# Turning the value tiles with one VectorE transpose and 24 ScalarE copies

## Chip, core and metric

The kernel runs on one core of a Trainium2 chip. The metric is the device time of one launch in microseconds; it is the median of the runs shown. PE is TensorE's matmul, PEld its weight load, DVE VectorE, ACT ScalarE, SP the engine that issues most DMAs.

## What is computed

One layer of a decoder trunk, for 256 new tokens of a prompt and for 8 sequences of 8 new tokens with a carried state: 320 tokens in all, model width 2048, fp32. Two token mixers read one input projection: A is an mLSTM with 4 heads (keys 256 wide, values 512), B an HGRN2 recurrence with 8 heads (keys 128, values 256). Cut to what matters here:

```python
proj = jnp.einsum('btd,de->bte', x, w_in)          # ml_q, ml_k, ml_v, ..., hg_q, hg_f, hg_i, hg_g, gate_a, gate_b
h, C, n, m = _mlstm(q, k, v, ig, lf, C0, n0, m0)   # num = (q k^T * d) v + w q C
branch_a = layernorm(h) * ml_norm_g * sigmoid(ml_o)
o, S = _hgrn2(hq, log f, 1 - f, hg_i, S0)          # o = a i + (q exp(G)) S
branch_b = rmsnorm(o) * hg_norm_g * silu(hg_g)
merged = sigmoid(gate_a) * (branch_a @ w_a) + sigmoid(gate_b) * (branch_b @ w_b)
x1 = layernorm(alpha * x + merged @ w_out)
y = layernorm(alpha * x1 + relu(x1 @ w_up)**2 @ w_down)
```

`v` and `hg_i` come out of the projection with channels on the partitions and tokens along the free dimension. The products with the score matrices need them with tokens on the partitions. That turn is what the change touches.

## The kernel before

**Projection stream.** All weights are cut into tiles of 128 output columns (`TILES`, L40): 40 tiles for the four heads of A (four `mv`, two `mk`, two `mq` and two gate tiles each), 4 gate tiles, 48 tiles for the eight heads of B (two gate tiles, `hf`, `hq` and two `hi` each), 16 `o` tiles, 4 gate tiles, then the branch, output and feed-forward tiles. A tile is two units of 8 blocks; each block is three matmuls of 320 columns (weights hi times x hi, hi times x lo, lo times x hi; L531 to L533), so a unit is 24 matmuls and a tile 48. The exact fp32 product is made of such hi and lo parts.

**Weight units.** SP loads a unit (128x1024) into `wr`. ACT rounds it to the hi part (L494, shown under the helper's line L350), DVE subtracts it to get the lo part (L497). There are three hi and lo buffers (`HL`), so a unit's conversion can start when PE has finished the unit three before it.

**Side work.** Everything else is done by chains: Python generators that yield one instruction at a time with an engine and a cost. While the program is built, a planner (`Sched`, L144 to L242) keeps a clock for each engine and lets a chain issue when its inputs are ready and the engine's queue is short. ACT and DVE instructions may be issued at most 0.9 us ahead of PE's clock; side matmuls go in between the projection's. So the costs in the program (`dve_t`, L269, is that of a transpose) set the order in which instructions stand on every engine, and nothing else: on the chip each engine works through its own row in order and waits only for real inputs.

**The turn.** `turn` (L1145) takes a value tile `x` (128 channels x n tiles x 320 tokens; n is 4 in A, `m_V` L948, and 2 in B, `h_i` L1474) and writes `to` with tokens on the partitions. A DVE transpose turns 32x32 blocks where they stand, so each group of 32 channel rows and 32 token columns must also change its partition quarter. Before, 24 transposes on 32 partitions do both: 16 for the prompt (L1156) and 8 for the sample tokens (L1159). Afterwards ACT and DVE make hi and lo parts of the turned values (L963 in A; L1487 and L1488 in B), and a matmul with `spread` copies the sample rows to where the state update needs them.

**Output rows.** In `h_out` (L1615) the two 128x256 halves of a head's prompt output are normalised, each is turned in place (L1631), and four DMAs write them home.

**The o tiles.** `ev_o` (L1691) makes branch A: the sigmoid of a tile read from its PSUM bank (L1309 to L1316), the product with the head output fetched from DRAM (L1698), then the split in hi and lo parts (L1672), the lo part into `ra`. In `ra`, the places for tile 7 and later are the same bytes that the last heads of B still use for their scan (`phl`) and their state update (`hkz0`). Three PSUM banks (`mbank`) take turns for the projection; ev_o holds one of two buffers (`sg`) from its first instruction to its split.

**Names in the rows.** `wh` and `wl` are hi and lo weights, `xh` and `xl` hi and lo x; `f`, `f3h`, `rx`, `ra`, `rxb`, `bb`, `rh` are big SBUF areas of which chains hold parts; `misc` holds single columns. Helpers give all ACT instructions the line L350 and most matmuls L356.

Of the kernel before, what the change touches and what calls it, by code (L numbers as in the profile page):

```python
# [20 lines left out]
TOK = 320  # L21
KT = 16
MH, DK, DV = 4, 256, 512
HH, HK, HV = 8, 128, 256
# [220 lines left out]
def wait(*evs):  # L245
    return ("wait", evs)


def acq(pool, n=1):
    return ("acq", pool, n)  # L250


def rel(pool, item):
    return ("rel", pool, item)


def post(ev):
    return ("set", ev)


def act(n, psum=False, ptr=0):
    return ((61 if psum else 112) + n) / 1.2 + 93 * ptr


def dve(n, psum=False, mode=1, ptr=0):
    return ((62 if psum else 66) + n / mode) / 0.96 + 55 * ptr


def dve_t(n):  # L269
    return 155.0 + 1.07 * n  # L270


def pe_f(n, m=128):
    return max(212.0 if m == 128 else 162.0, n * 1.66)
# [20 lines left out]
def by_row(ap, off, gap):  # L295

    return cap(ap, off, [[32, 4], [8, 2], [1, 8]] if gap else [[8, 4], [32, 2], [1, 8]])
# [16 lines left out]
class Program:  # L314
# [674 lines left out]
    def m_KW(self, h):  # L989
# [13 lines left out]
        m["khl"] = khl  # L1003
        kh, kl = khl[:, 0], khl[:, 1]
        yield ("dve", dve_t(512), lambda: v.transpose(kw[:, :, 0:256], kw[:, :, 0:256]))
        yield ("act", act(512), lambda: self.A(kh.rearrange("p s k -> p (s k)").rearrange("p (c t) -> p c t", c=2), kw[:, :, 0:256]))
        yield ("dve", dve(512), lambda: v.tensor_tensor(kl, kw[:, :, 0:256], kh.bitcast(F32), ALU.subtract))
# [56 lines left out]
    def m_num(self, h):  # L1064
# [14 lines left out]
        for i in range(2):  # L1079
            b = yield acq(self.sbank)  # L1080
            jobs = [(c, s) for c, s in (((0, 0),), ((128, 0), (256, 1)))[i]]
            n = 0
            for c, s in jobs:
                for x, w in ((sh, vh), (sh, vl), (sl, vh)):
                    st, sp = n == 0, n == 3 * len(jobs) - 1
                    yield ("pe", pe_r(512), lambda: self.mm(b, x[:, c:c + 128], w[:, s, :], start=st, stop=sp))
                    n += 1
            yield from self.ln_post(h, i, b, db[:, i:i + 1], hb[:, i, :], 128, True)
            yield rel(self.sbank, b)
            yield ("dve", dve_t(512), lambda: v.transpose(hb[:, i, :], hb[:, i, :]))  # L1090
# [54 lines left out]
    def turn(self, to, x):  # L1145

        v = self.nc.vector
        n = x.shape[1]
        for a in range(4):
            p = slice(32 * a, 32 * a + 32)  # L1150
            col = lambda y: y.rearrange("p (c a k) -> p a c k", a=4, k=32)[:, a]
            for b in range(4):
                q = slice(32 * b, 32 * b + 32)
                i = x[p, :, 0:NP_].rearrange("p c (i b k) -> p b i c k", b=4, k=32)[:, b]
                o = to[q, 0:2, :].rearrange("p i (c a k) -> p a i c k", a=4, k=32)[:, a]
                yield ("dve", dve_t(64 * n), lambda: v.transpose(o, i))  # L1156
            for b in range(2):
                o, i = col(to[64 + 32 * b:96 + 32 * b, 2, :]), x[p, :, NP_ + 32 * b:NP_ + 32 * b + 32]
                yield ("dve", dve_t(32 * n), lambda: v.transpose(o, i))  # L1159

    def later(self):
        e = Ev()
# [452 lines left out]
    def h_out(self, h):  # L1615
        nc, v, m = self.nc, self.nc.vector, self.hh[h]
        if h:
            yield wait(self.hh[h - 1]["o"])
        yield wait(m["aT"], m["I"])
        at, it = m["at"], m["it"]  # L1620
        on = yield acq(self.on)
        yield post(m["o"])
        b = yield acq(self.sbank)
        yield ("pe", pe_f(256), lambda: self.mm(b[:, 0:256], at[:, 0:128], it[:, 0, :], start=True, stop=True))
        yield ("pe", pe_f(256), lambda: self.mm(b[:, 256:512], at[:, 368:496], it[:, 0, :], start=True, stop=False))
        yield ("pe", pe_f(256), lambda: self.mm(b[:, 256:512], at[:, 128:256], it[:, 1, :], start=False, stop=True))
        for i in range(2):
            yield from self.rms(b[:, 256 * i:256 * i + 256], on[:, i, :], 128)
        yield rel(self.sbank, b)
        for i in range(2):  # L1630
            yield ("dve", dve_t(256), lambda: v.transpose(on[:, i, :], on[:, i, :]))  # L1631
        yield from self.place(self.rows_to(self.oH[h]), on[:, 0:2, :].rearrange("p i v -> p (i v)").rearrange("p (b c) -> p b c", c=32))
        done = self.later()
        yield wait(m["S"])
        ob = m["ob2"]
        yield from self.rms(ob[:, 0:256], on[:, 2, :], 128)
        yield rel(self.sbank, ob)
        yield rel(self.at, at)
        b = yield acq(self.sbank)
        for j in range(2):  # L1640
            yield ("pe", PE_T, lambda: nc.tensor.transpose(b[:, 128 * j:128 * j + 128], on[:, 2, 128 * j:128 * j + 128], self.ident))
        o = yield acq(self.ho)
        for j in range(2):
            yield ("act", act(64, True), lambda: self.A(by_row(o, 64 * j, False), by_row(b, 128 * j, True)))
        yield rel(self.sbank, b)
        yield ("sp", 620, lambda: self.dma(
            self.oL[h].rearrange("(j p) t -> p j t", p=128), o[:, 0:128].rearrange("p (j t) -> p j t", t=64)))
        for j in range(2):
            yield post(self.oT_ev[2 * h + j])
        yield wait(self.later())  # L1650
        yield rel(self.ho, o)
        yield wait(done)
        yield rel(self.on, on)
        yield wait(m["SP"], m["sdone"])
        yield rel(self.it, it)
        yield rel(self.hs, m["set"])
        yield post(m["end"])
# [33 lines left out]
    def ev_o(self, j, c, b):  # L1691
        v = self.nc.vector
        g = yield acq(self.sg)
        r = yield acq(self.sr)
        yield from self.sigmoid(b[:, :TOK], g, r, ((self.mbank, b),))
        yield rel(self.sr, r)
        x = yield from self.fetched("o", j)
        yield ("dve", dve(TOK, ptr=1), lambda: v.scalar_tensor_tensor(g, g, self.vec[:, V_MLG + j:V_MLG + j + 1], x, ALU.mult, ALU.mult))  # L1698
        yield rel(self.ld, x)
        yield from self.split(g, self.bah[:, j, :], self.bal[:, j, :])  # L1700
        yield rel(self.sg, g)
        yield post(self.ba_ev[j])
# [386 lines left out]
```

## Time and profile before

| | us |
|---|---|
| median of the runs shown | 2304.08 (2303.45 to 2305.43) |
| the profiled execution's own time | 2302.73 |
| its span | 2300.8 |
| PE busy | 2289.6 |
| PEld busy | 2246.1 |
| DVE busy | 1458.9 |
| ACT busy | 1036.6 |

The profile shows one execution. Busy times overlap: an instruction's duration runs from its start to its end, and the next can start before that end. An idle time stands with what ended it. The tables by stage split the span in stretches of 100 us. The stream's tile 0 starts at 5 us, the B heads' first tile at 385 us, the `o` tiles at 771 us and the `hg` tiles at 920 us.

### The profile page before, as it was taken

To read this page: it belongs to the slowest core of one execution; us is meant where nothing else is said; L and a number is where in the kernel's file an instruction comes from. 1 tells how busy PE (TensorE), PEld (TensorE's weight loads), DVE (VectorE), ACT (ScalarE), POOL (GpSimd) and SP (SyncE) were. 2 spreads that over 40 slices of the span, in tenths; PEclk is the share of its full clock that TensorE was granted. 3 is DMA by queue.
4 is the path that set the end of the run, shared out by engine and by line. 5 is a ranking of instruction groups with operands and counts; after the bars stand their busy time and mean duration, and the time that the engine had idled before them with its cause. 6 is when DMAs were issued, how large, how long until landed. Compare 5 with 4: busy or idle time off the path is not lost.

```text
span 2300.8 us, 38921 instructions
## 1 busy us (share of the span) xinstructions
PE 2289.6 (100%) x15592; PEld 2246.1 (98%) x15592; DVE 1458.9 (63%) x2634; ACT 1036.6 (45%) x1653; POOL 13.5 (1%) x37
## 2 busy tenths in 40 slices
PE   9999999999999999999999999999999999999998
PEld 9999899999999999999999999999999999999998
DVE  6786786788888886555555767654444444444455
ACT  5443445455555565444433446533433343234334
POOL 0000000000000000000000000000000000000000
PEclk9999999999999999999999999999999999999999
DMA  7667977755565564555545644444444444444475
GB/s 284 211 186 259 295 250 229 259 176 185 191 207 187 166 198 167 180 174 170 176 172 175 214 163 147 147 147 149 154 147 150 152 147 153 149 147 154 149 228 193
DMA packets 214574, 424.94 MB, mean 185 GB/s; under 512 B 83572, under 2 KB 110068, under 8 KB 213368
## 3 DMA queue, kind: packets, MB, share of 16 engines
q1 hardware_dynamic: 209512, 415.97, 53.7%
q0 software_dynamic: 4736, 6.29, 1.0%
q8 instruction: 122, 2.00, 0.3%
q14 instruction: 60, 0.49, 0.1%
q10 hardware_dynamic: 144, 0.20, 0.0%
HBM read 371.48 MB, written 50.90 MB: 184 GB/s over the span
## 4 chain that ended last, share of the span: by engine, by line
PE 69%; DVE 3%; ACT 1%; issue 0%; ACTq 0%; DVEq 0%
PE bank L356 69%; DVE wl L497 1%; ACT wh L350 0%; DVE f L1156 0%; DVE f L1445 0%; ACT f L350 0%; DVE f3m L1973 0%; DVE f3m L1980 0%; ACT f3m L350 0%; DVE f L1159 0%; DVE f L1315 0%; DVE f L1316 0%; DVE f L1631 0%; DVE f L1698 0%; DVE f L1309 0%
## 5 line engine op out<-in xcount | busy, mean ns | idle before, releaser
L356 PE MATMUL bank<-xh,wh 128*128 128x320 f32 (+1 forms) x2504 | 794.6, 318 | 0.0
L356 PE MATMUL bank<-xh,wl 128*128 128x320 f32 (+1 forms) x2504 | 774.8, 310 | 0.0
L356 PE MATMUL bank<-xl,wh 128*128 128x320 f32 (+1 forms) x2504 | 772.2, 309 | 0.0
L497 DVE TENSOR_TENSOR wl<-wr,wh 128x1024 fp32r<-128x1024 f32 x440 | 538.7, 1224 | 361.4 <-ACT wh L350 358.3
L350 ACT ACTIVATE wh<-wr 128x1024 fp32r<-128x1024 f32 x440 | 465.4, 1058 | 524.7 <-PE bank L356 495.6
L356 PEld LDWEIGHTS bank<-xh,wh 128*128 128x128 f32 x2504 | 472.0, 189 | 17.2 <-issue 15.3
L356 PEld LDWEIGHTS bank<-xl,wh 128*128 128x128 f32 x2504 | 471.5, 188 | 3.3
L356 PEld LDWEIGHTS bank<-xh,wl 128*128 128x128 f32 x2504 | 471.8, 189 | 0.2 <-DVE wl L497 0.2
L497 DVE TENSOR_TENSOR bb<-wr,bb 128x1024 fp32r<-128x1024 f32 x162 | 198.5, 1225 | 193.7 <-ACT bb L350 193.5
L350 ACT ACTIVATE bb<-wr 128x1024 fp32r<-128x1024 f32 x162 | 171.6, 1059 | 294.6 <-PE bank L356 277.5
L356 PE MATMUL bank<-ra,wh 128*128 128x320 f32 x1008 | 275.9, 309 | 0.7 <-DVE ra L1672 0.7
L356 PE MATMUL bank<-ra,bb 128*128 128x320 f32 x1096 | 255.2, 309 | 0.0
L356 PE MATMUL bank<-xh,bb 128*128 128x320 f32 (+1 forms) x1136 | 253.8, 309 | 0.0
L356 PE MATMUL bank<-rxb,bb 128*128 128x320 f32 x1088 | 249.0, 309 | 0.0
L356 PEld LDWEIGHTS bank<-xh,bb 128*128 128x128 f32 x1136 | 191.0, 188 | 0.0
L356 PE MATMUL bank<-rxb,wh 128*128 128x320 f32 x608 | 187.5, 308 | 0.0
L356 PE MATMUL bank<-rxb,wl 128*128 128x320 f32 x608 | 187.5, 308 | 0.0
L356 PEld LDWEIGHTS bank<-ra,bb 128*128 128x128 f32 x1096 | 184.9, 187 | 0.0
L356 PEld LDWEIGHTS bank<-rxb,bb 128*128 128x128 f32 x1088 | 184.2, 187 | 0.0
L356 PEld LDWEIGHTS bank<-ra,wh 128*128 128x128 f32 x1008 | 180.9, 187 | 0.9 <-DVE ra L1672 0.9
L356 PE MATMUL bank<-xl,bb 128*128 128x320 f32 (+1 forms) x568 | 175.5, 309 | 0.0
L356 PE MATMUL bank<-bb,wh 128*128 128x320 f32 (+1 forms) x536 | 119.0, 313 | 0.0
(259 smaller groups left out, 2244.4 us busy)
## 6 DMA issues: line engine op xcount, KB each, us to landing
wr<-wt SPq DMA_DIRECT2D x602, 512.0 KB, 3.3
rx<-C SPq DMA_DIRECT2D x34, 256.0 KB, 5.6
Cs<-rx SPq DMA_DIRECT2D x34, 256.0 KB, 4.8
f<-C SPq DMA_DIRECT2D x30, 256.0 KB, 5.5
Cs<-f SPq DMA_DIRECT2D x30, 256.0 KB, 4.1
f<-first SPq DMA_DIRECT2D x6, 704.0 KB, 9.6
vD<-ra SPq DMA_DIRECT2D x4, 1024.0 KB, 5.2
f<-S SPq DMA_DIRECT2D x8, 512.0 KB, 5.0
```

Source lines behind the costliest of these rows:

```text
L350: return self.nc.scalar.activation(out, in_, func, **kw)
L356: self.nc.tensor.matmul(*a, **kw)
L497: self.V().tensor_tensor(lo, raw, hi.bitcast(F32), ALU.subtract)
```

## The change

```diff
 def dve_t(n):
-    return 155.0 + 1.07 * n
+    return 295.0 + 1.05 * n
...
     def turn(self, to, x):
         v = self.nc.vector
         n = x.shape[1]
+        t = yield ("dve", dve_t(TOK * n), lambda: v.transpose(x, x))
         for a in range(4):
...
-                yield ("dve", dve_t(64 * n), lambda: v.transpose(o, i))
+                yield ("act", act(64 * n), lambda: self.A(o, i), (t,))
             for b in range(2):
                 o, i = col(to[64 + 32 * b:96 + 32 * b, 2, :]), x[p, :, NP_ + 32 * b:NP_ + 32 * b + 32]
-                yield ("dve", dve_t(32 * n), lambda: v.transpose(o, i))
+                yield ("act", act(32 * n), lambda: self.A(o, i), (t,))
...
-        for i in range(2):
-            yield ("dve", dve_t(256), lambda: v.transpose(on[:, i, :], on[:, i, :]))
+        yield ("dve", dve_t(512), lambda: v.transpose(on[:, 0:2, :], on[:, 0:2, :]))
...
         yield rel(self.ld, x)
+        if j > 6:
+            yield wait(self.hh[HH - 1]["aT" if j < 12 else "sdone"])
         yield from self.split(g, self.bah[:, j, :], self.bal[:, j, :])
```

The value tile is turned in place by one transpose over all 128 partitions (1280 columns in A, 640 in B), and ACT copies the 24 pieces to their quarters. The output rows of a head are turned by one transpose of 512 columns instead of two of 256. The planner's cost of a transpose is another. In `ev_o`, tiles 7 to 11 wait in the planner until the last head of B has its score matrix, tiles 12 to 15 until its state update is issued; this wait is of the planner alone, and puts the splits behind those instructions in the order. New lines move the later ones by 1, from L1698 on by 2.

Three places show the new order. First DVE, in B's head 5, the rows that end with L987, whose output a PE transpose (L1530) takes. Before:

```order
L497 TENSOR_TENSOR wl<-wr,wh 128x1024
L1323 TENSOR_SCALAR f3h<-f3h,misc 128x320
L1664 TENSOR_SCALAR misc<-misc 128x1
L1156 STREAM_TRANSPOSE f_76<-f_75 32x4x32
L1445 COPY_PREDICATED f_75<-lmask,bank_87 128x80
L1466 COPY_PREDICATED f_75<-lmask,bank_84 128x40x4
L1056 TENSOR_SCALAR misc<-misc 128x1
L1416 TENSOR_TENSOR f_75<-f_75 128x16x8
L1159 STREAM_TRANSPOSE f_76<-f_75 32x2x32
L1471 COPY_PREDICATED f_75<-lmask,bank_86 128x16x8
L1418 TENSOR_TENSOR f_75<-f_75 128x16x8
L987 TENSOR_TENSOR f_76<-f_75,f_76 128x16x8
```

The same place of the change, on DVE:

```order
L1467 COPY_PREDICATED f_75<-lmask,bank_86 128x40x4
L1664 TENSOR_SCALAR misc<-misc 128x1
L1446 COPY_PREDICATED f_75<-lmask,bank_87 128x80
L1056 TENSOR_SCALAR misc<-misc 128x1
L1420 TENSOR_TENSOR f_75<-f_75 128x40
L1310 TENSOR_SCALAR f_76<-bank_83 128x320
L497 TENSOR_TENSOR wl<-wr,wh 128x1024
L1059 TENSOR_TENSOR misc<-misc 128x1
L1060 TENSOR_TENSOR misc<-misc 128x1
L1417 TENSOR_TENSOR f_75<-f_75 128x16x8
L1472 COPY_PREDICATED f_75<-lmask,bank_88 128x16x8
L987 TENSOR_TENSOR f_76<-f_75,f_76 128x16x8
```

The pieces of the turn no longer stand between the scan's and the state's instructions.

Second ACT, from the 162nd weight conversion (`wh<-wr`) on, which is in the turn of B's head 5 in the change. Before, on ACT, up to the 164th:

```order
L350 ACTIVATE wh<-wr 128x1024
L350 ACTIVATE f_76<-bank_86,misc 128x256
L350 ACTIVATE wh<-wr 128x1024
L350 ACTIVATE f3h<-f3h 128x320
L350 ACTIVATE f3h<-f3h,misc 128x320 x2
L350 ACTIVATE wh<-wr 128x1024
```

The same place of the change, on ACT, up to the 163rd (32x4x32 and 32x2x32 are copies of the turn):

```order
L350 ACTIVATE wh<-wr 128x1024
L350 ACTIVATE f_75<-bank_84 32x32 x4
L350 ACTIVATE f_76<-f_75 32x4x32 x4
L350 ACTIVATE f3h<-f_75 128x128
L350 ACTIVATE f_76<-f_75 32x2x32 x2
L350 ACTIVATE f_76<-f_75 32x4x32 x4
L350 ACTIVATE wh<-wr 128x1024
```

Between two conversions stand ten copies that were not on ACT before.

Third DVE at the `o` tiles of the change, from the last state update of B's last head on; L1586 turns that head's keys, L1672 is the split of an `o` tile, L1310 the first reading of a later tile's bank:

```order
L1571 SCALAR_TENSOR_TENSOR f3h<-f3h,f_75,bank_87 128x256
L1417 TENSOR_TENSOR f_75<-f_75 128x2x64
L1419 TENSOR_TENSOR f_75<-f_75 128x2x64
L1420 TENSOR_TENSOR f_75<-f_75 128x2
L497 TENSOR_TENSOR wl<-wr,wh 128x1024
L1417 TENSOR_TENSOR f_75<-f_75 128x128
L1586 STREAM_TRANSPOSE f_75<-f_75 128x256
L1672 TENSOR_TENSOR ra<-f_76,rxb 128x320 x2
L1310 TENSOR_SCALAR f_76<-bank_83 128x320
```

The splits of tiles 7 and 8 stand together behind the head's last scan rows, and the bank of tile 9 is read behind them. On PE, counted in projection tiles from 0, the last head's scan now begins at tile 99.3 instead of 92.8, and its last state update stands at 102.2 instead of 98.6; `o` tile 7 is tile 99, so before, it came after both. The number of stretches of side matmuls between projection matmuls goes from 380 to 385.

## Prediction

> **What bounds the kernel now.** I read the busy shares first, then the table by stage, then PE's waits, then one wait in the timeline.
>
> ```profile
> span 2300.8 us, 38921 instructions
> PE 2289.6 (100%) x15592; PEld 2246.1 (98%) x15592; DVE 1458.9 (63%) x2634; ACT 1036.6 (45%) x1653; POOL 13.5 (1%) x37
> ```
>
> PE is busy in all but 11.2 us of the span, and the change takes no matmul away and adds none. So at most the idle time can be won. The table by stage tells where it is; its columns are the stretch and its length, then busy time and count of PE, PEld, DVE, ACT and POOL, PE's granted clock, the DMA share and GB/s.
>
> ```profile
> 100.00:200.00 100.00, 99.29 (x666) 92.78 (x665) 72.34 (x157) 42.86 (x70) 0.00 (x0) 1.00 0.66 214
> 200.00:300.00 100.00, 99.78 (x673) 92.54 (x672) 77.39 (x151) 43.32 (x72) 0.00 (x0) 1.00 0.82 265
> ...
> 500.00:600.00 100.00, 99.95 (x703) 97.28 (x702) 86.16 (x240) 56.01 (x123) 0.73 (x2) 1.00 0.62 197
> 600.00:700.00 100.00, 98.70 (x693) 96.08 (x693) 85.98 (x235) 55.73 (x124) 0.73 (x2) 1.00 0.59 190
> 700.00:800.00 100.00, 98.78 (x701) 95.22 (x700) 83.82 (x230) 57.19 (x129) 0.37 (x1) 1.00 0.56 180
> 800.00:900.00 100.00, 99.94 (x682) 99.24 (x681) 76.28 (x149) 60.77 (x113) 0.00 (x0) 1.00 0.57 181
> ...
> 2200.00:2300.00 100.00, 94.80 (x602) 91.36 (x600) 59.26 (x112) 38.91 (x63) 5.90 (x8) 0.99 0.70 221
> ```
>
> Of the 11.2 us, 5.2 lie in the last stretch, the closing layer norm, where nothing is changed. In the heads' stretches, 100 to 900, PE idles 0.71 + 0.22 + 0.05 + 1.30 + 1.22 + 0.06 = 3.56 us (none in 300 to 500). Most of it, 2.5 us, is between 600 and 800, where DVE is at 84 to 86% and ACT at 56%. PE's clock is full (0.99 in the last stretch). What ended PE's waits (total, times, longest):
>
> ```profile
> PE bank L1530 <- DVE f L987: 1.5, 3, 0.7
> PE bank L356 <- DVE rh L1488: 1.1, 2, 0.6
> PE bank L356 <- POOL ones L640: 1.0, 1, 1.0
> PE bank L1212 <- DVE f L1049: 0.7, 1, 0.7
> PE bank L356 <- DVE ra L1672: 0.7, 1, 0.7
> PE bank L356 <- DMA rx<-C: 0.2, 1, 0.2
> ```
>
> DVE ends six waits of the heads, 1.5 + 1.1 + 0.7 = 3.3 us of the 3.56; the L1672 row is at 1493 us, far behind the change, the POOL row at the start. One of them, first on DVE (start, duration), then on PE:
>
> ```profile
> 689.65 1.23 DVE L497 TENSOR_TENSOR wl<-wr,wh 128x1024 fp32r<-128x1024 f32 x1
> ...
> 697.65 0.30 DVE L1156 STREAM_TRANSPOSE f<-f 32x128 f32<-32x128 f32 x1
> ...
> 701.77 0.29 DVE L987 TENSOR_TENSOR f<-f,f 128x128 fp32r<-128x128 f32 x1
> ```
>
> ```profile
> 701.04 0.30 PE L356 MATMUL bank<-xl,wh 128*128 128x320 f32 x1
> 701.19 0.31 PE L356 MATMUL bank<-xh,wl 128*128 128x320 f32 x1
> 702.12 0.33 PE L1530 MATMUL bank<-cst,f 128*128 128x128 f32 x1 [0.62 <-DVE f L987]
> 702.20 0.39 PE L356 MATMUL bank<-xh,wh 128*128 128x320 f32 x1
> 702.43 0.32 PE L356 MATMUL bank<-xl,wh 128*128 128x320 f32 x1
> ```
>
> Projection matmuls start every 0.15 us. L1530 starts 0.93 us after the one before it, so this wait cost PE 0.93 - 0.15 = 0.78 us where 0.62 is shown as idle: hidden and shown stand as 1.26 to 1. DVE shows no idle time in the rows from 689.65 to L987, and pieces of the turn (L1156) stand in its queue ahead of L987.
>
> **The change part by part.** The pieces and their nearest rows (busy us, mean ns):
>
> ```profile
> L1156 DVE STREAM_TRANSPOSE f<-f 32x128 f32<-32x128 f32 x96 | 29.0, 303 | 2.3
> L1156 DVE STREAM_TRANSPOSE f<-f 32x256 f32<-32x256 f32 x64 | 27.9, 436 | 1.5
> L1159 DVE STREAM_TRANSPOSE f<-f 32x64 f32<-32x64 f32 x48 | 11.4, 238 | 1.0
> L1159 DVE STREAM_TRANSPOSE f<-f 32x128 f32<-32x128 f32 x32 | 9.7, 304 | 0.8
> L1156 DVE STREAM_TRANSPOSE f<-f3h 32x128 f32<-32x128 f32 x32 | 9.7, 302 | 0.7
> L1631 DVE STREAM_TRANSPOSE f<-f 128x256 f32<-128x256 f32 x16 | 7.0, 435 | 0.0
> L1090 DVE STREAM_TRANSPOSE f<-f 128x512 f32<-128x512 f32 x8 | 5.7, 709 | 0.2
> ...
> L1159 DVE STREAM_TRANSPOSE f<-f3h 32x64 f32<-32x64 f32 x16 | 3.8, 238 | 0.4
> ```
>
> *DVE, removed:* 16 x 436 + 8 x 304 = 9.4 us in a head of A, 16 x 303 + 8 x 238 = 6.8 us in one of B; over 4 and 8 heads 91.5 us. *Added:* a transpose takes 435 ns for 256 columns and 709 for 512, whatever the partitions, so 1.07 ns a column: 1.53 us for 1280 columns, 0.85 for 640, 12.9 us in all. No row has such a width; the bounds are 0.71 us (the 512 row) and 5 x 0.435 = 2.2 us for 1280, which moves DVE's sum by under 5 us either way. *Output rows:* 8 x (2 x 435 - 709) = 1.3 us less. Together DVE loses 80 us. In the B heads (386 us for 8) a head's DVE work falls by 6.1 us, 13 in 100: from 84 to 86 to some 72%.
>
> *ACT, added:* 288 copies. No row has a 32-partition copy within SBUF; by the rows of 64 partitions and equal columns:
>
> ```profile
> L350 ACT ACTIVATE rh<-f 64x256 fp32r<-64x256 f32 x8 | 3.3, 415 | 2.1 <-DVE f L1159 1.9
> L350 ACT ACTIVATE ra<-f 64x128 fp32r<-64x128 f32 x4 | 1.2, 308 | 0.1
> L350 ACT ACTIVATE f<-f 64x64 f32<-64x64 f32 x4 | 1.0, 253 | 0.9 <-DVE f L907 0.8
> ```
>
> A head of A takes 16 x 415 + 8 x 308 = 9.1 us, one of B 16 x 308 + 8 x 253 = 7.0 us, 92 us in all, and ACT goes from 56 to about 70% in the B heads. A lower bound of the 256-column copy is the 374 ns of the next nearest row, from PSUM, and there is no reason for less than that or for more than the 0.42 of the row taken:
>
> ```profile
> L350 ACT ACTIVATE ra<-bank 32x256 fp32r<-32x256 f32 x32 | 12.0, 374 | 5.5 <-PE bank L1530 5.1
> ```
>
> None of this lies on the path by itself: PE has 24 matmuls of 0.15 us, 3.6 us, in a unit, and two more units are converted ahead. What counts is how late a side matmul's input or a weight comes.
>
> *Waits that go.* The six waits ended by DVE have the queue of pieces ahead of them, or the turn itself (L1488 follows it). I take all of them away but one as long as the longest, 0.7 us, since the order is dealt anew everywhere: 3.3 - 0.7 = **-2.6 us**. The bounds are 0 (the waits come back elsewhere) and -3.56 x 1.26 = -4.5 us. With them gone the latest is the load of C states, of which PE shows 0.2 us:
>
> ```profile
> PEld bank L356 <- DMA rx<-C: 2.7, 5, 1.1
> PEld bank L356 <- ACT f3h L350: 0.9, 1, 0.9
> ```
>
> *Stretches of side matmuls.* 385 instead of 380; behind one the next projection matmul comes 0.23 us after the first instead of 0.15 (702.20 to 702.43), so 5 x 0.08 = **+0.4 us**.
>
> *Waits that come.* PE shows no wait ended by ACT, PEld one of 0.9 us that matters. The copies stand ahead of hi conversions and evacuations now. In the ACT rows shown with the change, the stretch between two conversions holds 4 bank copies (186 ns by their row), 8 copies of 308, 2 of 253, one of 128 columns and the conversion:
>
> ```profile
> L350 ACT ACTIVATE f<-bank 32x32 f32<-32x32 f32 x32 | 6.0, 186 | 1.8 <-PE bank L356 1.4
> L350 ACT ACTIVATE wh<-wr 128x1024 fp32r<-128x1024 f32 x440 | 465.4, 1058 | 524.7 <-PE bank L356 495.6
> ```
>
> That is 0.74 + 2.46 + 0.51 + 0.31 + 1.06 = 5.1 us by full durations, over PE's 3.6, and the two units ahead hide up to 7.2. So I take 0.2 us, nearest to the rows of today; the ends are 0 and 4.9 us (0.7 us, PE's longest wait, in seven of the twelve turns).
>
> *The planner's wait in ev_o* holds tiles 7 and 8 until the last head's scan is done, and the bank of tile 9 is read right behind them, by the order at about tile 102.9. PE needs that bank at tile 104, 1.1 tiles or 48 x 0.15 x 1.1 = 7.9 us later: nothing, and 1 us for each us beyond that if this cover is gone. SP issues as many DMAs as before.
>
> *Sum:* -2.6 + 0.4 + 0.2 = **-2.0 us**. The profiled execution took 2302.73 us, its span of 2300.8 and 1.9 around it; it would take 2300.7. The median of the runs is 1.35 us above that execution, so 2304.08 - 2.0 = **2302.1**.
>
> **One large transpose in place of 24 small ones.** The row that bears on it is that of the lo conversion:
>
> ```profile
> L497 DVE TENSOR_TENSOR wl<-wr,wh 128x1024 fp32r<-128x1024 f32 x440 | 538.7, 1224 | 361.4 <-ACT wh L350 358.3
> ```
>
> The Trainium skill, Perfetto Trace Analysis, section Optimizing Scalar/DVE Operations, says that where Scalar or Vector aren't saturated but cause bubbles on other engines, breaking instructions up can let work finish sooner; by that rule this edit goes the wrong way. The same section says that with DVE saturated, moving work to Scalar may make sense, which is for it. By rows: a 1.53 us transpose holds DVE 1.1 us longer than a piece of 0.44 did, but hardly longer than the 1.22 us that any lo conversion holds it, and PE shows no wait on L497. I count it at nothing; as a rival it stands below.
>
> **The rivals.** *(a) The waits only move*: both engines still end as many, since the planner deals a new order with the same margins. Then 2304.08 + 0.4 = 2304.5. For it: the order changes on all engines; against it: DVE is 13 points emptier. *(b) The large transposes block DVE*: 4 x 1.1 = 4.4 us in A's heads, 2306.5. Against it: see above, and DVE at 72 to 77% in the rows of A's heads. *(c) All waits go*, the hidden part too, and the C loads' weight waits with them: -4.5 - 2.5 + 0.4 = -6.6, 2297.5. Against it: nothing in the change touches the loads. *(d) ACT paces the turns*, the slower side: a turn's copies delay a hi conversion or the input of a side matmul beyond the margin, 0.7 us at each of 12 turns, 8.4 us with the 2.6 won: 2304.08 - 2.6 + 0.4 + 8.4 = 2310.3. It decides where ACT falls behind by more than the two units that are converted ahead, 7.2 us, or a side matmul's input by more than its margin; ACT at 70% speaks against the first. *(e) The last head is late*: if its scan comes 2.5 tiles later against PE than the order has it, 18 us, PE waits 18 - 7.9 = 10.1 us for a bank: 2302.1 + 10.1 = 2312.2. It decides from 1.1 tiles on; against it, DVE is emptier where that head works. That the change doesn't do what it says can't be: DVE's pieces are gone from the order.
>
> **How the numbers follow.** A measurement here can tell about 0.2%, 4.6 us: faster is below 2299.5, slower above 2308.7. Forecast 0.55, (a) 0.17, (b) 0.03, (c) 0.08, (d) 0.12, (e) 0.05. Same is the forecast, (a) and (b), 0.75; faster is (c), 0.08; slower is (d) and (e), 0.17. The range goes from (c), 2297.5, to the forecast with the upper end of new waits, 2302.1 - 0.2 + 4.9 = 2306.8, and leaves (d) and (e) out.
>
> **What would show it.** DVE busy near 1379 and ACT near 1129 us; L1149's transposes at 1.53 and 0.85 us; copies at 0.41, 0.31 and 0.25 us; DVE at about 72% between 500 and 800; PE's waits on L987, L1488 and L1049 nearly gone; PE idle between 100 and 900 near 1 us. Wrong it would be by waits of PE or PEld on ACT copies, on `wl`, or on a bank near the `o` tiles.

## The result and the profile after

| | us |
|---|---|
| before, median (4 runs) | 2304.67 (2303.45 to 2305.43) |
| after, median (4 runs) | 2315.99 (2314.73 to 2318.52) |
| ratio | 1.0051, 95% interval 1.0034 to 1.0068 |
| after, the profiled execution and its span | 2318.52, 2316.5 |

The change makes the kernel 0.5% slower. The forecast was 2302.1, in a range of 2297.5 to 2306.8; it started from 2304.08, the median of the first three of these runs of before. The loads came nearly as worked out, as the line of busy times on the page of the changed kernel shows:

```profile
PE 2294.2 (99%) x15592; PEld 2250.3 (97%) x15592; DVE 1368.2 (59%) x2350; ACT 1127.8 (49%) x1941; POOL 13.4 (1%) x37
```

So did the durations, in its groups of instructions by shape (busy us, mean ns of one):

```profile
L1149 DVE STREAM_TRANSPOSE f<-f 128x1280 f32<-128x1280 f32 x4 | 6.0, 1501 | 0.0
L1149 DVE STREAM_TRANSPOSE f<-f 128x640 f32<-128x640 f32 x6 | 5.0, 836 | 0.0
...
L350 ACT ACTIVATE f<-f 32x128 f32<-32x128 f32 x128 | 39.4, 307 | 6.0 <-DVE f L1420 2.6 <-DVE f L1149 1.7
L350 ACT ACTIVATE f<-f 32x256 f32<-32x256 f32 x64 | 26.6, 415 | 6.8 <-DVE f L1149 6.0
```

What is new stands in the table by stage (stretch, its length, busy time and count of PE, PEld, DVE, ACT and POOL, PE's granted clock, DMA share, GB/s):

```profile
400.00:500.00 100.00, 97.37 (x665) 92.43 (x664) 63.68 (x115) 57.85 (x120) 2.47 (x7) 0.98 0.65 213
500.00:600.00 100.00, 99.46 (x699) 96.96 (x698) 71.98 (x185) 66.75 (x167) 0.73 (x2) 1.00 0.59 182
600.00:700.00 100.00, 96.78 (x678) 94.03 (x677) 68.38 (x173) 66.22 (x161) 0.73 (x2) 1.00 0.58 188
700.00:800.00 100.00, 97.11 (x668) 94.29 (x667) 70.98 (x176) 65.22 (x154) 0.73 (x2) 0.98 0.60 186
800.00:900.00 100.00, 97.71 (x663) 95.80 (x662) 75.11 (x174) 66.63 (x154) 0.00 (x0) 0.98 0.59 179
```

DVE is at 64 to 75% there as forecast, and ACT nowhere above 67%. Yet PE idles 2.63 + 0.54 + 3.22 + 2.89 + 2.29 = 11.6 us in these five stretches, and in three of them its clock isn't full. PE's waits (total, times, longest) name ACT, and DVE instructions that come right behind an ACT copy:

```profile
PE bank L356 <- ACT f3h L350: 5.5, 2, 2.7
PE bank L356 <- DVE rh L1489: 5.0, 3, 2.6
PE bank L356 <- ACT f L350: 1.8, 4, 0.7
...
PE bank L356 <- DVE ra L964: 1.2, 1, 1.2
```

One of them in the timeline of the changed kernel, first ACT (start, duration, of `xN` the whole group), then PE:

```profile
743.30 1.27 ACT L350 ACTIVATE f<-f3h 32x128 f32<-32x128 f32 x4 [2.32 <-DVE f L1420]
744.59 0.31 ACT L350 ACTIVATE f3h<-f 128x128 f32<-128x128 f32 x1
744.92 0.25 ACT L350 ACTIVATE f<-f3h 32x64 f32<-32x64 f32 x1
745.20 1.06 ACT L350 ACTIVATE wh<-wr 128x1024 fp32r<-128x1024 f32 x1
746.29 5.15 ACT L350 ACTIVATE f<-f3h 32x64 f32<-32x64 f32 x17
751.46 1.06 ACT L350 ACTIVATE wh<-wr 128x1024 fp32r<-128x1024 f32 x1
752.42 0.45 ACT L350 ACTIVATE f<-f 128x320 f32<-128x320 f32 x1
752.90 0.52 ACT L350 ACTIVATE f<-f3h 32x64 f32<-32x64 f32 x2
...
754.78 0.29 ACT L350 ACTIVATE f3h<-f 128x128 f32<-128x128 f32 x1
```

```profile
752.10 0.31 PE L356 MATMUL bank<-xh,wl 128*128 128x320 f32 x1
755.13 0.49 PE L356 MATMUL bank<-f,f3h 128*128 128x128 f32 x2 [2.72 <-ACT f3h L350]
```

From 743.30 ACT never stands still. The 24 copies of a turn (4 + 1 + 17 + 2) go by without overlap: the 17 mixed ones take 5.15 us. Behind them, after four more ACT instructions, stands a 0.29 us copy to `f3h` (754.78) that a side matmul needs, and PE waits for it. Projection matmuls start every 0.15 us, so the 3.03 us from 752.10 to 755.13 cost PE 2.88.

By the starts of consecutive copies in the trace, a copy of 256, 128 or 64 columns is followed by the next after 427, 319 or 265 ns: 12 ns after its end. ACT instructions on all 128 rows overlap: the conversion that starts at 751.46 ends at 752.52, and the next instruction starts at 752.42. The planner counts every ACT instruction as if it overlapped: its cost `act(n)` is (112 + n) / 1.2 = 307, 200 and 147 ns. So it takes 16 x 200 + 8 x 147 = 4.4 us for a turn of B, where the chip needs 16 x 319 + 8 x 265 = 7.2. ACT is 2.85 us later behind a turn than the order of the program was made for.

**Theory 1** is that: the copies don't overlap, the planner believes that they do, and side matmuls stand in PE's row up to 2.9 us too early. **Rival 1** is that any other dealt order costs about so much. **Rival 2** is that 92 us more are too much for ACT where the turns are.

### The profile page after: what moved, and what is told of

It is laid out like the page before. It is cut to its first block, busy times and chain, and to the rows that moved or that the text cites. A ratio compares the mean times of both kernels' runs of the same rounds, so it can differ in the third digit from the quotient of the medians.

```text
span 2316.5 us, 38923 instructions
## 1 busy us (share of the span) xinstructions
PE 2294.2 (99%) x15592; PEld 2250.3 (97%) x15592; DVE 1368.2 (59%) x2350; ACT 1127.8 (49%) x1941; POOL 13.4 (1%) x37
## 4 chain that ended last, share of the span: by engine, by line
PE 93%; ACT 3%; DVE 1%; DMA 1%; issue 1%; SPq 0%; ACTq 0%; DVEq 0%
PE bank L356 93%; ACT f L350 2%; ACT wh L350 1%; DMA rx<-C 1%; DMA Cs<-rx 0%; SPq L359 0%; DVE wl L497 0%; DMA f<-first 0%; DVE f3m L1975 0%; DVE f3m L1982 0%; ACT f3h L350 0%; ACT f3m L350 0%; DVE f L1149 0%; ACT ra L350 0%; PE bank L1027 0%
## 5 line engine op out<-in xcount | busy, mean ns | idle before, releaser
L350 ACT ACTIVATE f<-f 32x128 f32<-32x128 f32 (+6 forms) x413 | 152.8, 370 | 39.7 <-DVE f L1310 19.9
```

What stands on the lines that cost most here:

```text
L350: return self.nc.scalar.activation(out, in_, func, **kw)
```

## The experiments

Twelve kernels, each timed beside the kernel before. In the table, "extra" is what the planner counts more for each copy of the turn; the ratio is against the kernel before.

| kernel | median us | ratio, 95% interval |
|---|---|---|
| the change with extra 60 ns | 2306.13 | 1.0008, 0.9999 to 1.0017 |
| extra 100 ns | 2299.71 | 0.9980, 0.9971 to 0.9989 |
| extra 120 ns | 2298.29 | 0.9977, 0.9967 to 0.9986 |
| extra 140 ns | 2301.79 | 0.9989, 0.9979 to 0.9998 |
| extra 240 ns | 2309.64 | 1.0024, 1.0014 to 1.0034 |
| the change with the turn's loops exchanged | 2318.18 | 1.0059, 1.0044 to 1.0074 |
| the change in B's turns alone | 2317.30 | 1.0055, 1.0040 to 1.0070 |
| before, with the new cost of a transpose alone | 2302.44 | 0.9995, 0.9986 to 1.0005 |
| before, with the new output rows and the wait in `ev_o` | 2305.03 | 1.0000, 0.9990 to 1.0009 |
| extra 120 ns but for pairs on the same rows | 2298.00 | 0.9974, 0.9963 to 0.9985 |
| extra 120 ns, transpose at its measured cost | 2298.91 | 0.9976, 0.9967 to 0.9986 |
| probe of the rows (one run) | 2302.99 | |

**The copies at their true cost.**

```diff
-                yield ("act", act(64 * n), lambda: self.A(o, i), (t,))
+                yield ("act", act(64 * n) + 120, lambda: self.A(o, i), (t,))
...
-                yield ("act", act(32 * n), lambda: self.A(o, i), (t,))
+                yield ("act", act(32 * n) + 120, lambda: self.A(o, i), (t,))
```

> The change as it is, but the planner counts each of the 24 copies of a turn at 120 ns more (427, 320 and 267 ns), which is about the step that the profile of the change shows between two of them (427, 319 and 265 ns). Theory 1 (the copies do not overlap with one another, the planner believes that they do, ScalarE runs about 24 x 0.12 = 2.9 us late at the end of every turn, and the inputs of side matmuls that stand behind it come up to 2.9 us late): the copies still step 427, 319 and 265 ns, but TensorE's three waits of about 3 us are gone, its waits that end on ScalarE's f3h and on VectorE's rh fall from 10.5 us to under 2, the granted clock stays full until the end, and the time is 2301 to 2306 us. Rival 1 (any other dealt order costs some 10 us): 2306 to 2320 us with waits in other places. Rival 2 (ScalarE's added 92 us of work are too much for it where the turns are): the waits stay, 2312 to 2318 us.

It took 2298.29 us, 17.7 less than the change and 5.9 less than the kernel before. That is 2.7 us below the range that I gave for theory 1, so the gain was more than I expected. PE's waits, all of them, and the two worst stretches of the change:

```profile
PE bank L356 <- POOL ones L640: 1.0, 1, 1.0
PE bank L356 <- DVE ra L1672: 0.7, 1, 0.7
PE bank L356 <- DVE rh L1489: 0.7, 2, 0.4
PE bank L356 <- DVE rx L1272: 0.2, 1, 0.2
```

```profile
600.00:700.00 100.00, 100.00 (x704) 97.85 (x703) 72.11 (x180) 70.34 (x172) 0.73 (x2) 1.00 0.63 190
700.00:800.00 100.00, 100.00 (x703) 97.69 (x702) 74.68 (x186) 69.30 (x166) 0.73 (x2) 1.00 0.65 194
```

Same work, ACT even fuller (70% instead of 66), and PE doesn't idle at all. This rules out rival 2. A number in the plan was worth 17.7 us.

**Too dear a copy.** The same edit with 240 in place of 120.

> As the run with 120 ns more for each copy, with 240 ns (547, 440 and 387 ns), which is more than the copies take. Theory 1: what counts is that ScalarE isn't later than planned, so it is as good as with 120 ns within 3 us: 2301 to 2306 us, no wait of TensorE over 1.5 us on ScalarE's outputs. Rival 1 (any other order costs): another time again, 2306 to 2320 us. Rival 2 (load): 2312 to 2318 us.

This missed theory 1's 2301 to 2306 us: 2309.64. The long waits on the copies are gone, as expected, but another is there. PE's longest wait, and PE around it:

```profile
PE bank L356 <- DVE f L1419: 5.0, 1, 5.0
```

```profile
847.55 0.31 PE L356 MATMUL bank<-xh,wl 128*128 128x320 f32 x1
...
857.58 1.12 PE L356 MATMUL bank<-f 128*128 128x64 f32 x4 [5.03 <-DVE f L1419]
...
869.86 0.42 PE L356 MATMUL bank<-xh,wh 128*128 128x320 f32 x1 [0.33 <-DVE f L1310]
```

No projection matmul starts between 847.55 and 869.86; counted from the start, the next one is the first of tile 104. That is the place of the prediction's rival (e): the bank for tile 104 comes free behind the wait in `ev_o`, which needs the last head of B. With copies planned too dear the side work is dealt later, PE gets through the projection faster (tile 92 at 751 us, with 120 ns at 759), and the last head is late against it. So a cost may be too high as well as too low.

**The cost of a transpose alone**, in the kernel before.

```diff
-    return 155.0 + 1.07 * n
+    return 295.0 + 1.05 * n
```

> The kernel before with one line of the change alone: the planner's cost of a VectorE transpose (295 + 1.05 n instead of 155 + 1.07 n); the turn stays VectorE's 24 transposes, and the output rows are turned in two. The dealt order is another one, and no work goes to ScalarE. Theory 1: like the kernel before, 2303 to 2306 us, no wait of TensorE near 3 us and the clock full. Rival 1 (any other dealt order costs some 10 us): 2310 us or more.

2302.44 us, just below the 2303 to 2306 expected: another order on every engine, and no loss. That speaks against rival 1. PE's waits in the heads show one thing more:

```profile
PE bank L356 <- DMA rx<-C: 1.9, 2, 1.0
...
PE bank L356 <- ACT rh L350: 0.3, 1, 0.3
```

None of the six waits that the prediction wanted to win (on L987, L1488 and L1049) is left, though the pieces of the turn are still on DVE. Another dealt order was enough for that.

**What keeps copies from overlapping.** A probe that leaves out the change of quarter: A's copies stay in their own quarter, B's take all 128 rows.

```diff
+                if n == 4:
+                    o = to[p, 0:2, :].rearrange("p i (c a k) -> p a i c k", a=4, k=32)[:, b]
+                else:
+                    i = x[:, :, 0:NP_].rearrange("p c (i b k) -> p b i c k", b=4, k=32)[:, b]
+                    o = to[:, 0:2, :].rearrange("p i (c a k) -> p a i c k", a=4, k=32)[:, a]
...
+                if n == 4:
+                    o = col(to[p, 2, :])
+                else:
+                    o, i = col(to[:, 2, :]), x[:, :, NP_ + 32 * b:NP_ + 32 * b + 32]
```

> A probe of what keeps the copies from overlapping; the values are turned wrongly on purpose, so the output isn't the reference's. In the turn of 4 pieces (n = 4) each copy reads and writes the same 32 rows, without a shift to another quarter; in the turn of 2 pieces each copy takes all 128 rows with the same number of elements a row. If a copy on a part of the rows doesn't overlap with the next (theory 1a), the first still step by 427 and 319 ns or so and the second step by about 95 ns less than their duration. If the shift from one quarter to another does it (1b), the first overlap too. If it is the strided pattern of the elements (1c), neither overlaps. The time should be 2304 to 2318 us and tells little.

The planner's costs are those of the change, and the program's order on PE and DVE is the same instruction by instruction, but for one pair of matmuls that stand next to each other in the trace. Eleven and twelve copies of one turn of A, in the change and then in the probe:

```profile
208.53 4.35 ACT L350 ACTIVATE f<-f 32x256 f32<-32x256 f32 x11
214.46 4.68 ACT L350 ACTIVATE f<-f 32x128 f32<-32x128 f32 x12
```

```profile
203.38 3.41 ACT L350 ACTIVATE f<-f 32x256 f32<-32x256 f32 x11
208.36 3.73 ACT L350 ACTIVATE f<-f 32x128 f32<-32x128 f32 x12
```

Copies that stay on one set of 32 rows step 308 ns at a duration of 402. Where the next one goes to another set, they still step 321 at 309, without a shift in either. So neither (1a), a part of the rows, nor (1b), the shift, nor (1c), the pattern of the elements, is right as I had put it. What goes with the missing overlap is that the next copy stands on other rows than the last. (B's copies overlap, 216 at 310, where the next one writes another place. Most of them write the same place again in my probe; those start 32 ns after the end of the last, and not 12.) In this one run the time is 2302.99 us, 13 less than the change **in the same order** and below the 2304 to 2318 expected, and PE's waits shrink with the copies:

```profile
PE bank L356 <- ACT f3h L350: 3.0, 2, 1.5
PE bank L356 <- DVE rh L1498: 2.9, 2, 1.6
```

As far as one run shows, that finishes rival 1: the order that costs 11 us with slow copies costs nothing with faster ones.

**Which rows, read or written?** The loops of the turn are exchanged, so that the quarter written to stays for four copies.

```diff
-        for a in range(4):
-            p = slice(32 * a, 32 * a + 32)
...
-            for b in range(4):
-                q = slice(32 * b, 32 * b + 32)
+        for b in range(4):
+            q = slice(32 * b, 32 * b + 32)
+            for a in range(4):
+                p = slice(32 * a, 32 * a + 32)
...
+        for b in range(2):
+            for a in range(4):
+                p = slice(32 * a, 32 * a + 32)
...
```

> The change with the loops of the turn exchanged: the four copies that write to one quarter of the partitions stand one behind the other (b outside, a inside), and the quarter that they read changes each time. Costs as in the change (307 and 200 ns). In the probe, copies that stayed on one set of 32 rows stepped 306 ns at a duration of 402, and those that went from one set to the next did not overlap. Theory 1, with the quarter written to as what counts: 18 of the 23 steps of a turn overlap (about 308 ns in A, 200 in B), ScalarE is at most 0.7 us late behind a turn, TensorE's waits of 3 us are gone, 2298 to 2305 us. Theory 1 with the quarter read as what counts, or with both: the steps stay at 427, 319 and 265 ns, waits of about 3 us, 2308 to 2318 us. Rival 1 (any other order costs): 2306 to 2320 us whatever the steps.

The steps stay at 427, 319 and 265 ns, and the time is 2318.18 us, 0.2 us above what was expected for this case. A change of the rows read is enough, as a change of the rows written was in the other order. PE waits of the same kind and size stand in another order:

```profile
PE bank L356 <- DVE rh L1491: 4.3, 2, 2.6
PE bank L356 <- ACT f L350: 3.5, 2, 2.0
```

**Half the missing cost.** 60 in place of 120.

> The change with 60 ns more for each copy in the planner, half of what it lacks. Theory 1: ScalarE is late by 24 x 0.06 = 1.4 us behind a turn instead of 2.9; TensorE's longest waits on ScalarE's f3h and VectorE's rh are 1.0 to 1.7 us, none of them takes the clock down, and the time lies between the change (2316.0) and the version with 120 ns (2298.3): 2301 to 2309 us. Rival 1 (each order has its own luck): no relation to the cost, anywhere from 2298 to 2316 us, with waits in other places.

2306.13 us, between the change and 120 ns as theory 1 has it; the clock stayed full. PE's longest waits behind the copies are down to 0.9 (`rh`), 1.4 (`f3h`, L1571, the state update) and 0.5 us (ACT `f`); the longest of all is 1.8 on L987.

**Which turns?** The change in B's turns alone; A's pieces are as before.

```diff
-        t = yield ("dve", dve_t(TOK * n), lambda: v.transpose(x, x))
+        t = (yield ("dve", dve_t(TOK * n), lambda: v.transpose(x, x))) if n == 2 else None
...
-                yield ("act", act(64 * n), lambda: self.A(o, i), (t,))
+                if n == 2:
+                    yield ("act", act(64 * n), lambda: self.A(o, i), (t,))
+                else:
+                    yield ("dve", 155.0 + 1.07 * 64 * n, lambda: v.transpose(o, i))
...
```

> The change in the eight turns of B alone (two pieces, 128x640), A's four turns as before on VectorE with their old cost. Theory 1: the three waits near 3 us of the change are in the stretch of B's heads (from 385 to 850 us) and stay, 2 to 4 of them with 2.0 to 3.1 us each, and the granted clock falls behind those that leave TensorE idle for more than half of 3.4 us; A's share (the waits at 64, 170 and 186 us, 4.7 us) goes: 2306 to 2314 us. Rival 1: 2300 to 2316 us, waits elsewhere.

2317.30 us, 3 above what I expected. The waits in B's stretch are the same to the tenth:

```profile
PE bank L356 <- ACT f3h L350: 5.5, 2, 2.7
PE bank L356 <- DVE rh L1495: 5.0, 3, 2.6
```

A's waits are gone, but they had been worth little: this execution comes to B's heads at 382.6 us, the change at 385.2, and the medians lie the other way round by 1.3 us. The loss of the change is B's.

**Output rows and the wait in `ev_o` alone.** The kernel before with these two edits.

```diff
-        for i in range(2):
-            yield ("dve", dve_t(256), lambda: v.transpose(on[:, i, :], on[:, i, :]))
+        yield ("dve", dve_t(512), lambda: v.transpose(on[:, 0:2, :], on[:, 0:2, :]))
...
+        if j > 6:
+            yield wait(self.hh[HH - 1]["aT" if j < 12 else "sdone"])
```

> The kernel before with the output rows of a head of B turned in one VectorE operation, and with the planner's wait ahead of the splits of the o tiles, nothing else; the turn and the cost of a transpose are the old ones. Theory 1 and rival 2: nothing to be seen, 2302 to 2306 us. Rival 1 (any other dealt order costs): 2310 us or more.

2305.03 us, ratio 1.0000: nothing to be seen.

**Is 120 ns an accident?** 100 and 140 in its place.

> The change with 100 ns more for each copy in the planner (407, 300 and 247 ns; the steps on the chip are 427, 319 and 265). Theory 1: ScalarE is at most 24 x 0.02 = 0.5 us late behind a turn, no wait of TensorE near 2 us on its outputs, clock full: 2297 to 2304 us, so that the gain at 120 ns is no accident of one order. If the order's luck decides more than the lateness: 2304 to 2316 us.

> The change with 140 ns more for each copy (447, 340 and 287 ns), a little more than the steps. Theory 1: 2297 to 2304 us, waits as with 120 ns. If the side work comes later with each added cost, and the last head with it (what the 5 us wait at 852 us of the version with 240 ns shows): a first sign of it is a stretch without projection matmuls near 850 us; 2304 to 2310 us then.

With 100 ns 2299.71 us. With 140 ns 2301.79 us, inside the range, and with the sign that was named: in its profile the projection pauses from 856.4 to 860.43 us, at tile 104 again, and PE waits 1.6 us for L1310, which reads the bank. The granted clock is at half for the 3.41 us behind that, from 860.30. The best cost lies where ACT is just not late.

**Pairs on the same rows.** The two sample copies of a quarter go right behind the prompt copy between the same rows.

```diff
-                yield ("act", act(64 * n), lambda: self.A(o, i), (t,))
-            for b in range(2):
-                o, i = col(to[64 + 32 * b:96 + 32 * b, 2, :]), x[p, :, NP_ + 32 * b:NP_ + 32 * b + 32]
-                yield ("act", act(32 * n), lambda: self.A(o, i), (t,))
+                yield ("act", act(64 * n) + (0 if b > 1 else 120), lambda: self.A(o, i), (t,))
+                if b > 1:
+                    o, i = col(to[q, 2, :]), x[p, :, NP_ + 32 * (b - 2):NP_ + 32 * (b - 2) + 32]
+                    yield ("act", act(32 * n) + 120, lambda: self.A(o, i), (t,))
```

> The change with the two sample copies of a quarter put right behind the prompt copy that goes from the same rows to the same rows; the planner counts the first of such a pair at the old 307 and 200 ns and every other copy at 120 ns more. In the probe, copies without a shift overlapped where rows read and rows written stayed the same. If a change of the rows is what keeps copies from overlapping: the first of each of the eight pairs of a turn, though it shifts by one to three quarters, steps about 310 to 320 ns in A at a duration of 402 to 415, and 200 to 220 ns in B at 308; all else steps 427, 319 and 265 ns; ScalarE isn't late, 2297 to 2304 us. If the shift itself does it: the pairs step 427 and 319 ns, ScalarE is 8 x 0.12 = 1 us late behind a turn, waits of 1 us come, 2300 to 2307 us.

The first of a pair steps 323 ns at a duration of 414 in A and 216 at 307 in B, with a shift of up to three quarters; all others step 12 ns after their end. So it is the change of rows, and not the shift. 2298.00 us is the best version of all, 6.2 us under the kernel before, though not to be told from 120 ns for all copies.

**The transpose at its measured cost.** 120 ns for the copies, and:

```diff
-    return 295.0 + 1.05 * n
+    return 185.0 + 1.03 * n
```

> The change with both costs set to what the profile shows: copies at 120 ns more, VectorE's transpose at 185 + 1.03 n (1503 and 844 ns at 1280 and 640 elements; the profile has 1501 and 836) instead of 295 + 1.05 n (1639 and 967). Theory 1: the transposes' extra 0.13 us in the plan gave slack that nothing needed; as with 120 ns alone, 2296 to 2303 us. If the plan was held by that slack: waits of TensorE on VectorE's outputs come back, 2303 to 2308 us.

2298.91 us: the transpose's cost decides nothing.

## Why the prediction was wrong, step by step

**The step that failed is "Waits that come", taken as 0.2 us with ends of 0 and 4.9.** It saw that the copies stand ahead of conversions and of the inputs of side matmuls, summed a stretch of ACT by full durations (5.1 us), and let "the two units ahead" cover it with 7.2 us. Those units cover late weights: PE shows no wait for `wh` or `wl` in the changed kernel either. They cover no input of a side matmul. That has only the planner's clock, and the planner had 200 ns where the same section used 308. In place of 0.2 us, or 4.9 at most, PE's waits on the copies' outputs and on what stands behind them came to 5.5 + 5.0 + 1.8 + 1.2 = 13.5 us, in lumps of up to 2.7, and the sum had no term at all for what such a lump does to PE's clock. I had the row and the code, and never set one against the other. A duration alone wouldn't have shown it, since most ACT durations are longer than their planned cost and overlap; the step was to be read, and the trace of the kernel before has it where 32-row instructions follow one another:

```profile
662.71 0.79 ACT L350 ACTIVATE f<-bank 32x32 f32<-32x32 f32 x4 [0.80 <-PE bank L356]
```

Four instructions of 186 ns in 0.79 us step 0.20: no overlap. They read a PSUM bank, where the copies read SBUF. In that whole trace, of 35 pairs of 32-row ACT instructions that follow one another within 0.06 us none overlapped, and of 783 pairs on 128 rows 542 did. By the step and the planner's cost a turn of B is late by 2.85 us, close to what the wait at 752 us took (2.88).

**What the lost time is made of.** Up to 900 us PE idles 16.0 us in the changed kernel by the table by stage, and 4.5 in the kernel before: 11.5 more. The rest is the clock. Periods of 3.41 us around three long waits, and around one without consequence (647 to 654), in the changed kernel:

```profile
473.24:476.66 3.42, 0.79 (x6) 0.68 (x6) 2.37 (x4) 2.40 (x4) 0.00 (x0) 1.00 0.46 151
476.66:480.07 3.41, 3.41 (x15) 3.41 (x15) 2.54 (x4) 1.93 (x3) 0.00 (x0) 0.50 0.53 193
647.32:650.74 3.42, 1.82 (x13) 1.55 (x11) 1.44 (x3) 3.29 (x9) 0.00 (x0) 1.00 0.00 0
650.74:654.15 3.41, 2.27 (x16) 2.27 (x17) 1.93 (x4) 2.94 (x9) 0.00 (x0) 1.00 0.50 154
753.14:756.55 3.41, 1.42 (x10) 1.42 (x11) 1.98 (x5) 3.27 (x10) 0.00 (x0) 1.00 0.47 151
756.55:759.96 3.41, 3.41 (x15) 3.41 (x14) 3.36 (x8) 0.46 (x3) 0.00 (x0) 0.50 0.34 86
821.40:824.82 3.42, 1.55 (x10) 1.25 (x10) 3.36 (x8) 1.83 (x5) 0.00 (x0) 1.00 0.72 174
824.82:828.23 3.41, 3.41 (x15) 3.41 (x15) 2.04 (x7) 3.27 (x9) 0.00 (x0) 0.50 0.71 228
```

Three times the granted clock is 0.50 for one period. Matmuls then start every 0.267 us instead of 0.147, which by my estimate costs 3.41 x (1 - 0.147 / 0.267) = 1.5 us, 4.6 in all. 11.5 + 4.6 = 16.1, and the two profiled executions differ by 2318.52 - 2302.73 = 15.8. The medians differ by only 11.3; the profiled execution is the slowest of the four after.

**The other steps.** *DVE and ACT:* ACT rose by 91.2 us (92 worked out). DVE's busy time fell by 90.7 where the durations gave 80. The sum of all DVE durations in the two traces does fall by 80.1 (1548.8 to 1468.6). The other 10.6 is time in which two neighbours overlap, counted once in busy time: 100.5 us instead of 89.9. The 32-row pieces had hardly any of it: in the kernel before, 19 of 465 pairs of a 32-row and a 128-row DVE instruction overlapped, none of 38 pairs on 32 rows, and 1048 of 1252 on 128 rows.

*Waits that go:* the size was right, and seen once the copies are costed right: of the 3.3 us on L987, L1488 and L1049 0.7 is left with 120 ns, just the 3.3 - 0.7 = 2.6 of the sum. The reason, a DVE queue without the pieces, is not shown: with the new cost of a transpose alone these waits are gone too, and PE idles 0.34 us between 500 and 800 instead of 2.57, with DVE still at 83 to 84% there. That kernel gains 1.75 us by the medians, which its interval doesn't tell from nothing. The whole gain with 120 ns is 5.9 us, near rival (c), which takes the hidden part and the weight waits for C loads too (2.7 us before, 0.5 + 0.9 with 120 ns). How much of it the emptier DVE earned, and how much another dealt order, wasn't separated.

*The large transpose, counted at nothing:* the three versions near 2298 us hold DVE with the same transposes, and PE has no wait of a microsecond on DVE in the heads there. The rule of the Trainium skill, Perfetto Trace Analysis, section Optimizing Scalar/DVE Operations, on breaking instructions up, set against the row in the prediction, has no case here.

*The planner's wait in `ev_o`:* nothing by itself, as forecast; but its cover, 7.9 us at tile 104, is used up with 140 ns and far overrun with 240. Rival (e) was a real place that the change doesn't reach. *Stretches of side matmuls*, 0.4 us: not tried apart.

**The rivals.** (d) is what happened, by the second half of its condition (a side matmul's input late by more than its margin). Its price was wrong: 0.7 us at each of 12 turns, where it is 2 to 3 us at four places and the clock on top. Its chance, 0.12, rested on ACT's 70%; load was the wrong thing to ask.

## What to carry to other kernels

Where a planner deals the order, compare its cost for each moved instruction with the **step** between two of them in the trace; an error of 0.12 us, 24 times in a row, was worth 17.7 us here, and too high a cost does harm as well. Ask of every input that queues behind moved work what cover it has: buffers that are filled ahead cover weights, and nothing covers a side matmul that the plan has put in PE's row. Busy shares don't show this: ACT was at 66% with the waits and at 70% without them.

## What the runs showed of the hardware

**ACT copies of 32 rows overlap with the next on the same rows only.** In the changed kernel's trace, of 279 pairs of 32-row instructions that follow one another within 0.06 us none overlapped (the next starts 12 ns after the end), and of 780 pairs on 128 rows 550 did, by 95 ns at the median of all. Copies on the same 32 rows overlapped by 91 to 93 ns, with a shift (the pairs) or without (the probe). Between sets of unequal size the runs don't show the condition: 16 of 118 pairs of a 32-row and a 128-row instruction overlapped in the changed kernel, so equal rows aren't needed there. The Trainium skill, ScalarE: Activation LUTs, section What ACT_TABLE_LOAD costs, says that back-to-back ACTIVATEs overlap by about 93 ns; the runs agree for a constant set of rows, and not where 32-row copies change it.

**A wait of 2 us can halve PE's clock for 3.41 us, if it falls well.** All changes of the granted clock in an execution lie on one grid of 3.413 us (476.658 to 756.551 us in the changed kernel are 82.00 of it), which starts elsewhere in each. Across the runs and ahead of the closing layer norm, nine such periods at full clock with 1.87 to 2.69 us of PE idle were each followed by one at half clock, and every one at full clock with 1.85 us or less by another at full clock. The change in B's turns alone has both sides close together (idle 2.07, then 1.85 us):

```profile
645.84:649.25 3.41, 1.34 (x10) 1.07 (x8) 1.91 (x4) 3.27 (x10) 0.00 (x0) 1.00 0.00 0
649.25:652.67 3.42, 2.75 (x11) 2.75 (x12) 1.94 (x4) 2.49 (x7) 0.00 (x0) 0.50 0.48 153
...
751.65:755.07 3.42, 1.57 (x11) 1.30 (x9) 1.70 (x4) 3.27 (x9) 0.00 (x0) 1.00 0.00 0
755.07:758.48 3.41, 2.53 (x18) 2.53 (x19) 1.93 (x3) 2.70 (x8) 0.00 (x0) 1.00 0.46 154
```

So 3.05 us from one matmul's start to the next that the grid cuts in two (648.8 us in the changed kernel, idle 1.60 and 1.14) cost nothing more, and 2.17 us inside a period (822.4 us, idle 1.87) did. The Trainium skill, TensorE: Matmul & The Clock Gate, Part 1, has the free-running window of 3413 ns, with which this agrees. It says that the clock falls after an idle window, and to avoid idle gaps above about 3.4 us; here somewhat over half a window idle was enough. For the way back the same traces have 13 periods at half clock. The nine with 0.13 us or less of PE idle were followed by full clock, and the four with 0.15 us or more by another at half: 0.67 us in the change in B's turns alone, and 2.34, 0.36 and 0.15 with 240 ns, where the clock stayed at half for four periods (13.65 us from 855.24). These are few cases, and no run was made to try this.
